# Last two experts added by one-hot products instead of scattered rows, in the tail of a hybrid decoder layer

## The chip, the cores and the metric

The kernel runs on one core of a Trainium2 chip. The metric is the device time in microseconds (us) of one execution. TensorE is called PE below, VectorE DVE, ScalarE ACT, GpSimd POOL and SyncE SP. SP only issues transfers here. "Span" is the time from the first to the last instruction in the profile.

## The reference

One decoder layer over 1024 tokens of width 1024: differential attention and latent attention side by side, cross attention to 256 memory tokens, and a mixture of 32 experts of which each token takes two, all with residual adds, and a final RMSNorm. The change touches only how the experts' rows come back to their tokens, and the final norm:

```python
def block_fn(args):
    tok, wt, e = args
    xb = h_pad[tok]
    hidden = jax.nn.silu(xb @ w_gate[e]) * (xb @ w_up[e])
    return (hidden @ w_down[e]) * wt[:, None].astype(hf.dtype)
...
out = jnp.zeros((n_tok + 1, d), hf.dtype).at[slot_token].add(y.reshape(n_slots, d))[:n_tok]
...
x = x + _hierarchical_moe(...)
return _rms_norm(x, norm_final_g)
```

So the output of a token is the norm of its residual row plus two weighted expert rows.

## The kernel before

All work is recorded first and then ordered by a scheduler written in Python (`Sched`), which emits the instructions of each engine; every scheduled instruction therefore shows the one line L524 (L525 after the change) in the trace, and is told by its tile names. Large tiles (128 rows of 1024 floats, `t4`) share one pool of 50 buffers, and PE writes to 8 PSUM banks.

The experts run one after the other. For expert `e`, POOL gathers the 96 rows of its tokens from DRAM (`xg<-XN,gidx`), PE transposes them and makes the gate and up products (`m_gu`), the hidden rows are transposed (`m_h`), and `m_d` makes the down product of 96 rows by 1024 columns in two banks. ACT scales each bank by the token's weight into the tile `y`, and POOL scatters `y` to a DRAM table `Y` of 2048 rows, two for each token (first and second choice). A scatter waits until the scatter before it has landed, since both write `Y`. The weights come as float32 tiles `eraw`, are split into a high part `ehi` by ACT and a low part `elo` by DVE, and each product is three matmuls in float32r (high by high, high by low, low by high). A plain float32 matmul is used for the first experts' hidden rows (`hw`).

After the last expert `m_end` loads the eight residual tiles (`yt<-XR`). Then the recorded work is flushed and the program comes to an `If` on a count `nov`, of tokens beyond 96 in an expert. With this input `nov` is zero, and the block under the `If` is skipped. Behind it stands the tail: the gain `gfin`, and 16 loads `yt<-Y`, of 512 KB each, the first- and second-choice rows `y0` and `y1` of each of the eight token tiles. The loads go over eight queue semaphores in turn, and SP issues one when the load eight before it has landed. For each tile POOL (tiles 0 to 5) or DVE (6 and 7) adds `y0` to the residual `z`, DVE adds `y1`, ACT squares and sums the row, DVE makes the inverse root in twelve tiny operations for a group of tiles (`rsqrt_mean`, tile `ss`), multiplies by it and by the gain (`scalar_tensor_tensor`), and SP stores the tile.

Of the kernel before, what the change touches and what calls it, by code (L numbers as in the profile page):

```python
# [12 lines left out]
F32 = mybir.dt.float32  # L13
F32R = mybir.dt.float32r
BF16 = mybir.dt.bfloat16
I32 = mybir.dt.int32
AF = mybir.ActivationFunctionType
OP = mybir.AluOpType
# [4 lines left out]
P = 128  # L23
D = 1024
S = 1024
KT = D // P
NT = S // P
# [9 lines left out]
NG, NEG_, NE, FF = 4, 8, 32, 256  # L37
# [18 lines left out]
WHOLE_GU = range(0)  # L56
WHOLE_D = range(4)
WHOLE_PV = ()
TAIL = ((0, 1), (2, 3), (4, 5), (6,), (7,))
TAILV = (6, 7)  # L60
PARK = range(8)
NPRE = 0
NXG = 3
# [10 lines left out]
NS = 96  # L74
# [452 lines left out]
def f32(t):  # L527
    return t.bitcast(F32)
# [30 lines left out]
def hybrid_kernel(ctx: ExitStack, tc: tile.TileContext, a, out):  # L559
    nc = Sched(tc.nc)  # L560
    ctx.enter_context(tc.manual_schedule())
    mm = nc.tensor.matmul

    def mm3(o, ah, al, bh, bl, start, stop):
        mm(o, ah, bh, start=start, stop=False)
        mm(o, ah, bl, start=False, stop=False)
        mm(o, al, bh, start=False, stop=stop)

    def sb(stack, name, bufs=1, side="left"):
        return nc.pool(stack, tc, name, bufs, side=side, reuse_waits="tile")  # L570
# [3 lines left out]
    sm = sb(ctx, "sm")  # L574
# [4 lines left out]
    def bank():  # L579
        return ps.tile([P, 512], F32, tag="b", name="bank", bufs=8)  # L580
# [8 lines left out]
    def t4(name, *shape, dt=F32):  # L589
        v = big.tile(list(shape) or [P, 1024], dt, tag="t4", name=name, bufs=N4)  # L590
        if name == "eraw":
            v.tile.reserve = RESERVE_M
        if name in ("ehi", "elo", "xT", "xw", "hid", "hw", "sg", "y"):
            v.tile.reserve = RESERVE_W
        return v
# [20 lines left out]
    ident = hc[:, 32:160]  # L616
    iota_f = hc[:, 160:288]
# [10 lines left out]
    r = 0  # L628
# [46 lines left out]
    Y = dram.tile([2 * S, D], F32, name="Y")  # L675
# [17 lines left out]
    def two(name):  # L693

        return t4(name, P, 2, CH, dt=F32R)
# [504 lines left out]
    wsl = keep.tile([P, NE], F32, name="wsl")  # L1200
    gidx = keep.tile([P, NE], I32, name="gidx")

    sidx = sums.rearrange("p t h -> p (t h)")[:, 0:NE].bitcast(I32)
# [454 lines left out]
        nc.vector.tensor_copy(nov, obend[:, NE - 1:NE])  # L1658


    w_g, w_u, w_d = (a[n].rearrange("o e d f -> (o e) d f") for n in ("w_expert_gate", "w_expert_up", "w_expert_down"))
    pieces = {}

# [25 lines left out]
    def moe_load(e):  # L1689
        for j in range(6):  # L1690
            moe_piece(e, j)
# [56 lines left out]

    def m_d(e):
        h = st[e]["h"]  # L1750
        y = t4("y")
        for n in range(2):
            yp = bank()
            for k in range(2):
                sl = slice(k * NS, (k + 1) * NS)
                if e in WHOLE_D:
                    mm(yp[0:NS], h[:, 0, sl], pieces[e, 4 + k][:, n], start=k == 0, stop=k == 1)
                else:
                    wh, wl = st[e][4 + k]
                    mm3(yp[0:NS], h[:, 0, sl], h[:, 1, sl], wh[:, n], wl[:, n], k == 0, k == 1)  # L1760
            nc.scalar.activation(y[0:NS, n * 512:(n + 1) * 512], yp[0:NS], AF.Copy, scale=wsl[0:NS, e:e + 1])
        nc.gpsimd.indirect_dma_start(out=Y[:, :], out_offset=Rows(ap=sidx[0:NS, e:e + 1], axis=0), in_=y[0:NS],
                                     in_offset=None, bounds_check=2 * S - 1, oob_is_err=False)

    ys = []

    def m_end():

        for t in range(NT):
            ys.append([t4("yt")])  # L1770
            nc.sync.dma_start(ys[t][0], XR[t * P:(t + 1) * P])
            nc.hold(ys[t][0])

    def experts():
        for e in range(NE + 1):
            if e < NE:
                for i in range(AHEAD):
                    moe_load(e + i)
                m_x(e)
                for j in range(4):  # L1780
                    m_split(e, j)
                moe_load(e + AHEAD)
                if e > 0:
                    m_h(e - 1)
                m_gu(e)
                for j in range(4, 6):
                    m_split(e, j)
            if e > 0:
                if e == NE:
                    m_end()  # L1790
                    m_h(e - 1)
                m_d(e - 1)
# [92 lines left out]
    lazy, nc = nc, tc.nc  # L1885
    mm = nc.tensor.matmul
    A_, obst_, obend_, rank_, nov_, hc_, w3_, XN_, Y_ = (v.real() for v in (A, obst, obend, rank, nov, hc, w3, XN, Y))
# [6 lines left out]
    with tc.If(rnov > 0):  # L1894
# [37 lines left out]
        n = 0  # L1932
        for t in range(NT):
            for k in range(2):
                oh = ohs[n % 2]
# [30 lines left out]
        with tc.For_i(0, rnov, 1) as b:  # L1966
            ev = nc.sync.value_load(bei[0:1, bass.ds(b, 1)], min_val=0, max_val=NE - 1)
            ix = take(1, 2, dt=I32)
            nc.vector.tensor_copy(ix, oidx[:, :, bass.ds(b, 1)].rearrange("p a o -> p (a o)"))
            wx = take(1, 1)  # L1970
            nc.vector.tensor_copy(wx, ow[:, bass.ds(b, 1)])
            wgu = [r4("wgu", P, 2, 512) for _ in range(4)]
            wdn = [r4("wdn") for _ in range(2)]
            for i in range(4):
                for src, o in ((w_g, 0), (w_u, 256)):
                    nc.sync.dma_start(wgu[i][:, :, o:o + 256], src[bass.ds(ev, 1)].rearrange(
                        "o (p k) f -> p (o k) f", k=KT)[:, 2 * i:2 * i + 2])
            for i in range(2):
                nc.sync.dma_start(wdn[i], w_d[bass.ds(ev, 1), i * P:(i + 1) * P].rearrange("o p f -> p (o f)"))
            xg = r4("oxg")  # L1980
            nc.vector.memset(xg, 0.0)
            nc.gpsimd.indirect_dma_start(out=xg, out_offset=None, in_=XN_[:, :],
                                         in_offset=bass.IndirectOffsetOnAxis(ap=ix[:, 1:2], axis=0),
                                         bounds_check=S - 1, oob_is_err=False)
            xT = r4("oxT")
            for g in range(2):
                xp = rbank()
                for k in range(4):
                    o = (4 * g + k) * P
                    nc.tensor.transpose(xp[:, k * P:(k + 1) * P], xg[:, o:o + P], ident_)  # L1990
                nc.vector.tensor_copy(xT[:, g * 512:(g + 1) * 512], xp)
            gu = rbank()
            for k in range(KT):
                mm(gu, xT[:, k * P:(k + 1) * P], wgu[k // 2][:, k % 2], start=k == 0, stop=k == KT - 1)
            sg = take(1, FF)
            nc.scalar.activation(sg, gu[:, 0:FF], AF.Silu)
            nc.vector.tensor_mul(sg, sg, gu[:, FF:2 * FF])
            hp = rbank()
            for k in range(2):
                nc.tensor.transpose(hp[:, k * P:(k + 1) * P], sg[:, k * P:(k + 1) * P], ident_)  # L2000
            hT_ = take(1, 2 * P)
            nc.vector.tensor_copy(hT_, hp[:, 0:2 * P])
            y = r4("oy")
            for n in range(2):
                yp = rbank()
                for k in range(2):
                    mm(yp, hT_[:, k * P:(k + 1) * P],
                       wdn[k][:, n * 512:(n + 1) * 512], start=k == 0, stop=k == 1)
                nc.vector.tensor_scalar(y[:, n * 512:(n + 1) * 512], yp, wx, None, op0=OP.mult)
            nc.gpsimd.indirect_dma_start(out=Y_[:, :], out_offset=bass.IndirectOffsetOnAxis(ap=ix[:, 0:1], axis=0), in_=y,  # L2010
                                         in_offset=None, bounds_check=2 * S - 1, oob_is_err=False)
    nc = lazy


    gf = t4("gfin")
    nc.sync.dma_start(gf, a["norm_final_g"].partition_broadcast(P))
    y_t = Y.rearrange("(t p k) d -> t k p d", p=P, k=2)
    o_t = out.rearrange("o (t p) d -> (o t) p d", p=P)
    for t in range(NT):
        for k in range(2):  # L2020
            ys[t].append(t4("yt"))
            nc.sync.dma_start(ys[t][1 + k], y_t[t, k])

    for tiles in TAIL:
        n = len(tiles)
        ss = carve("ss1")(3, n)
        for i, t in enumerate(tiles):
            z, y0, y1 = ys[t]
            (nc.gpsimd if t not in TAILV else nc.vector).tensor_add(z, z, y0)
            nc.vector.tensor_add(z, z, y1)  # L2030
            nc.scalar.activation(y0, z, AF.Square, accum_out=ss[:, 0, i:i + 1])
        rsqrt_mean(ss[:, 2], ss[:, 0], D, ss[:, 1])
        for i, t in enumerate(tiles):
            z = ys[t][0]
            nc.vector.scalar_tensor_tensor(z, z, ss[:, 2, i:i + 1], gf, op0=OP.mult, op1=OP.mult)
            nc.sync.dma_start(o_t[t], z)
            nc.drop(z)


_INS = ["x", "mem", "positions", "norm_mix_g", "w_in", "diff_lambda_q1", "diff_lambda_k1", "diff_lambda_q2",  # L2040
# [21 lines left out]
```

## Time and profile before

| what | value |
|---|---|
| median of 3 runs | 1236.42 us (1232.04 to 1237.33) |
| profiled execution, its own time | 1232.18 us |
| its span | 1230.0 us |
| mean granted PE clock | 0.945 of full |
| PE, DVE, ACT, POOL busy | 89%, 73%, 65%, 35% of the span |
| bytes moved | 264.95 MB, mean 215 GB/s |

The busy shares are means over stages that differ: PE is nearly always busy until 1166 us and does nothing in the last 64 us. Sums below are made against the span; the profiled execution lies 4.24 us under the median of the runs.

### The profile page before, as it was taken

The numbers are of one execution on the slowest core, as the hardware profiler recorded it, in microseconds if no ns is written. First come the engines' busy times: TensorE is split into PE (matmuls) and PEld (weight loads), VectorE is DVE, ScalarE is ACT, GpSimd is POOL, SyncE is SP. The second block draws the span as 40 slices with busy tenths as digits, with TensorE's granted clock in tenths as the row PEclk, the third lists the DMA queues.
The fourth block names the chain that finished last, engine by engine and source line by source line (L and its number), as shares of the span: only waits on it lengthen the run. The fifth ranks groups of instructions, "written<-read, shape, count | busy, mean of one in ns | idle before, by whom it ended". The sixth has DMA issues, their size and how long they took to land. (4 is left out here: it accounts for less than half of the span.)

```text
span 1230.0 us, 19697 instructions
## 1 busy us (share of the span) xinstructions
PE 1089.7 (89%) x6285; PEld 895.1 (73%) x6285; DVE 895.2 (73%) x2066; ACT 795.8 (65%) x1597; POOL 427.5 (35%) x384
## 2 busy tenths in 40 slices
PE   3999999998788999988999999995999999999800
PEld 2998898897666887678999888884566777766500
DVE  5947535368899879998482566876577889989648
ACT  5735327489888789987362464652676888889702
POOL 2214321158837456957211002153132222221150
PEclk9999999999899999899999999895998999999955
DMA  9118898359845562555440232786999999999983
GB/s 297 34 50 296 309 374 257 123 155 265 198 111 137 143 170 67 136 154 182 155 157 17 69 103 77 254 272 215 326 311 326 339 333 341 342 344 380 365 298 137
DMA packets 147419, 264.95 MB, mean 215 GB/s; under 512 B 17291, under 2 KB 65778, under 8 KB 147314
## 3 DMA queue, kind: packets, MB, share of 16 engines
q1 hardware_dynamic: 131264, 216.61, 55.1%
q0 software_dynamic: 15680, 46.75, 10.9%
q8 instruction: 50, 0.82, 0.3%
q14 instruction: 55, 0.45, 0.1%
q10 hardware_dynamic: 370, 0.32, 0.1%
HBM read 216.96 MB, written 55.05 MB: 221 GB/s over the span
## 5 line engine op out<-in xcount | busy, mean ns | idle before, releaser
L524 DVE TENSOR_TENSOR elo<-eraw,ehi 128x1024 fp32r<-128x1024 f32 x182 | 218.1, 1229 | 36.0 <-ACT ehi L524 28.8
L524 ACT CAST ehi<-eraw 128x1024 fp32r<-128x1024 f32 x184 | 187.2, 1052 | 4.5 <-DMA eraw<-in_w_expert_up_dram 1.9
L524 PE MATMUL bank<-ehi,xT 128*96 128x512 f32 x512 | 170.3, 404 | 2.0 <-ACT y L524 0.5
L524 PE MATMUL bank<-k,q 128*128 128x512 f32 (+5 forms) x480 | 131.0, 383 | 8.4 <-DVE mx L524 2.1
L524 DVE TENSOR_TENSOR pT<-bank,pT 128x512 fp32r<-128x512 f32 (+2 forms) x208 | 108.9, 560 | 24.4 <-ACT pT L524 23.9
L524 PE MATMUL acc<-pT,v 128*128 128x512 f32 (+3 forms) x384 | 114.9, 381 | 11.0 <-DVE pT L524 5.4
L524 PEld LDWEIGHTS bank<-ehi,xT 128*96 128x96 f32 x512 | 83.8, 164 | 39.6 <-ACT y L524 5.7
L524 ACT CAST pT<-bank 128x512 fp32r<-128x512 f32 (+2 forms) x208 | 92.7, 497 | 29.2 <-PE bank L524 28.2
L524 POOL DMA_INDIRECT Y<-y,sums x32 | 36.9, 1154 | 205.3 <-ACT y L524 172.3
L524 PE MATMUL bank<-hc,pt 128*128 128x128 f32 x640 | 98.2, 282 | 10.1 <-POOL pt L524 7.7
L524 PEld LDWEIGHTS bank<-k,q 128*128 128x128 f32 (+1 forms) x480 | 83.9, 198 | 26.1 <-DVE mx L524 8.0
L524 PE MATMUL bank<-elo,xT 128*96 128x512 f32 x256 | 102.0, 399 | 0.3 <-DVE elo L524 0.2
L524 PE MATMUL lbank<-whi,mix 128*128 128x256 f32 x512 | 97.0, 286 | 0.0
L524 PEld LDWEIGHTS bank<-hc,pt 128*128 128x128 f32 x640 | 76.9, 144 | 21.7 <-POOL pt L524 8.7
L524 PE MATMUL lbank<-whi,hT 128*128 128x256 f32 (+1 forms) x384 | 86.7, 311 | 0.0
L524 PEld LDWEIGHTS acc<-pT,v 128*128 128x128 f32 x384 | 65.9, 196 | 27.9 <-DVE pT L524 11.9
L524 PEld LDWEIGHTS lbank<-whi,mix 128*128 128x128 f32 x512 | 81.3, 192 | 0.2
L524 PE MATMUL lbank<-hT,whi 128*128 128x512 f32 x256 | 81.1, 395 | 0.0
L524 PE MATMUL bank<-ehi,hid 128*96 128x512 f32 x224 | 74.7, 394 | 0.8 <-ACT hid L524 0.8
L524 PE MATMUL lbank<-wlo,mix 128*128 128x256 f32 x256 | 72.5, 283 | 0.0
L524 DVE TENSOR_REDUCE mx<-bank 128x1 f32<-128x512 f32 (+3 forms) x112 | 61.0, 568 | 14.7 <-PE bank L524 14.4
L524 POOL TENSOR_TENSOR O<-O,sh 64x512 f32<-64x512 f32 x32 | 41.8, 1307 | 78.4 <-ACT O L524 68.2
(625 smaller groups left out, 2710.1 us busy)
## 6 DMA issues: line engine op xcount, KB each, us to landing
eraw<-in_w_expert_gate_dram SPq DMA_DIRECT2D x128, 256.0 KB
eraw<-in_w_expert_up_dram SPq DMA_DIRECT2D x128, 256.0 KB
eraw<-in_w_expert_down_dram SPq DMA_DIRECT2D x64, 512.0 KB
k<-KD SPq DMA_DIRECT2D x72, 128.0 KB
QM<-st POOLq DMA_DIRECT2D x16, 512.0 KB, 6.4
q<-QM SPq DMA_DIRECT2D x16, 512.0 KB
wraw<-in_w_out_dram SPq DMA_DIRECT2D x16, 512.0 KB
yt<-Y SPq DMA_DIRECT2D x16, 512.0 KB
```

The costliest lines, as they stand in the source:

```text
L524: getattr(getattr(self.nc, eng), name)(*[real(v) for v in a], **{n: real(v) for n, v in k.items()})
```

## The change

Experts 30 and 31 no longer scatter. `m_d` keeps their rows in SBUF as `yl`, a high part (ACT) and a low part (DVE). For each of the two experts and each of the eight token tiles DVE builds a one-hot matrix `oh` (96 rows by 128 tokens, one where the row's token stands), and in the tail PE adds these rows by products of `oh` with `yl`: two experts by two parts by two halves of 512 columns, 8 products for a tile. For the tiles in `TAILP` (1, 3, 4, 6, 7) PE also adds `y0` and `y1`, by float32 products with an identity matrix, 4 more; for tiles 0, 2 and 5 DVE adds them as before. DVE then adds each bank (128 by 512) to the residual. POOL adds nothing in the tail. Since the places of experts 30 and 31 in `Y` are read all the same, `y_zero` writes zeros to them: it is recorded at expert 10, a zeroed tile and two scatters. The 16 loads of `Y` and that of `gfin` stand in `m_end` now, ahead of the `If`; under the `If` the 16 tiles are loaded a second time, since that block writes to `Y`. The tiles are normed in three groups, no longer in five.

```diff
-TAIL = ((0, 1), (2, 3), (4, 5), (6,), (7,))
-TAILV = (6, 7)
+NLAST = 2
+TAIL = ((0, 1), (2, 3, 4), (5, 6, 7))
+TAILP = (1, 3, 4, 6, 7)
...
     def m_d(e):
         h = st[e]["h"]
-        y = t4("y")
+        y = t4("y") if e < NE - NLAST else None
...
-            nc.scalar.activation(y[0:NS, n * 512:(n + 1) * 512], yp[0:NS], AF.Copy, scale=wsl[0:NS, e:e + 1])
+            w = wsl[0:NS, e:e + 1]
+            if e >= NE - NLAST:
+                yl = last[e, n] = two("yl")
+                nc.scalar.activation(yl[0:NS, 0], yp[0:NS], AF.Copy, scale=w)
+                nc.vector.scalar_tensor_tensor(yl[0:NS, 1], yp[0:NS], w, f32(yl[0:NS, 0]), op0=OP.mult, op1=OP.subtract)
+                nc.hold(yl)
+            else:
+                nc.scalar.activation(y[0:NS, n * 512:(n + 1) * 512], yp[0:NS], AF.Copy, scale=w)
+        if e >= NE - NLAST:
+            return
...
+    def y_zero():
+
+        z = t4("y")
+        nc.gpsimd.memset(z[0:NS], 0.0)
+        for e in range(NE - NLAST, NE):
+            nc.gpsimd.indirect_dma_start(out=Y[:, :], out_offset=Rows(ap=sidx[0:NS, e:e + 1], axis=0), in_=z[0:NS],
+                                         in_offset=None, bounds_check=2 * S - 1, oob_is_err=False)
 
     def m_end():
 
         for t in range(NT):
             ys.append([t4("yt")])
             nc.sync.dma_start(ys[t][0], XR[t * P:(t + 1) * P])
-            nc.hold(ys[t][0])
+        for t in range(NT):
+            for k in range(2):
+                ys[t].append(t4("yt"))
+                nc.sync.dma_start(ys[t][1 + k], y_t[t, k])
+            nc.hold(*ys[t])
+        for e in range(NE - NLAST, NE):
+            g = sm.tile([P, 1 + NT], F32, name="lastg", bufs=2)
+            nc.vector.tensor_copy(g[0:NS, 0:1], gidx[0:NS, e:e + 1])
+            oh = last[e] = t4("oh", P, NT, P, dt=F32R)
+            for t in range(NT):
+                nc.vector.tensor_scalar(g[0:NS, 1 + t:2 + t], g[0:NS, 0:1], -float(t * P), None, op0=OP.add)
+                nc.vector.tensor_scalar(oh[0:NS, t], iota_f[0:NS], g[0:NS, 1 + t:2 + t], None, op0=OP.is_equal)
+            nc.hold(oh)
+        last["gf"] = t4("gfin")
+        nc.sync.dma_start(last["gf"], a["norm_final_g"].partition_broadcast(P))
+        nc.hold(last["gf"])
 
     def experts():
         for e in range(NE + 1):
+            if e == 10:
+                y_zero()
...
+        y_t_ = Y_.rearrange("(t p k) d -> t k p d", p=P, k=2)
+        for t in range(NT):
+            for k in range(2):
+                nc.sync.dma_start(ys[t][1 + k].real(), y_t_[t, k])
     nc = lazy
...
             z, y0, y1 = ys[t]
-            (nc.gpsimd if t not in TAILV else nc.vector).tensor_add(z, z, y0)
-            nc.vector.tensor_add(z, z, y1)
+            if t not in TAILP:
+                nc.vector.tensor_add(z, z, y0)
+                nc.vector.tensor_add(z, z, y1)
+            for b in range(2):
+                po = bank()
+                h = slice(b * 512, (b + 1) * 512)
+                m = [(last[e][0:NS, t], last[e, b][0:NS, x]) for e in range(NE - NLAST, NE) for x in range(2)]
+                if t in TAILP:
+                    m = [(ident, y0[:, h]), (ident, y1[:, h])] + m
+                for x, (l, r) in enumerate(m):
+                    mm(po, l, r, start=x == 0, stop=x == len(m) - 1)
+                nc.vector.tensor_add(z[:, h], po, z[:, h])
             nc.scalar.activation(y0, z, AF.Square, accum_out=ss[:, 0, i:i + 1])
```

On SP, at the end of the program before the change, the residual loads are followed by the branch (L1893, L1894), and only behind it stand the gain and the `Y` loads; `DMAHW0` to `DMAHW7` are the eight queue semaphores, `DMASW6` that of a scatter:

```order
L524 DMA yt<-XR 128x1024 [waits DMAHW5_49,DVE_49]
L1893 TENSOR_LOAD nov [waits DVE_49]
L1893 ISA x2
L1894 COMPARE_AND_BRANCH
...
L1894 UNCONDITIONAL_BRANCH [waits SP_sequencer_49,DMAHW0_49,DMAHW1_49,DMAHW2_49,DMAHW3_49,DMAHW4_49,DMAHW5_49,DMAHW6_49,DMAHW7_49]
L524 DMA gfin<-in_norm_final_g_dram 128x1024 [waits DMAHW0_49,DVE_49]
L524 DMA yt<-Y 128x1024 [waits DMASW6_49,DMAHW1_49,DMASW0_49,PE_49]
L524 DMA yt<-Y 128x1024 [waits DMAHW2_49,DVE_49]
```

The same place after it; the rows L2053 are the second loads under the `If`:

```order
L525 DMA yt<-XR 128x1024 [waits DMAHW5_49,DVE_49]
L525 DMA gfin<-in_norm_final_g_dram 128x1024 [waits DMAHW6_49,DVE_49,PE_49]
L525 DMA yt<-Y 128x1024 [waits DMAHW7_49,DMASW6_49,DVE_49]
L525 DMA yt<-Y 128x1024 [waits DMAHW0_49,PE_49]
...
L525 DMA yt<-Y 128x1024 [waits DMAHW6_49,PE_49]
L1931 TENSOR_LOAD nov [waits DVE_49]
...
L2053 DMA yt<-Y 128x1024 x8
...
L1932 UNCONDITIONAL_BRANCH [waits SP_sequencer_49,DMAHW0_49,DMAHW1_49,DMAHW2_49,DMAHW3_49,DMAHW4_49,DMAHW5_49,DMAHW6_49,DMAHW7_49]
L525 DMA out_dram<-yt 128x1024 [waits DMAHW1_49,DVE_49]
```

The 16 loads have moved ahead of the branch and behind one scatter (of expert 29) only. The last branch row is what SP does when the block is skipped: it waits for each queue's own loads, one queue after the other, and then raises that queue's semaphore by what the skipped loads would have added. In the built program the tail's first readers wait for the raised counts: DVE's first add for that of `DMAHW1`, PE's first identity product for those of `DMAHW3` and `DMAHW1`.

PE has nothing behind the branch before the change; after it, these are its first rows there (`yl,oh` a one-hot product, `yt,hc` an identity product):

```order
L525 MATMUL bank<-yl,oh 128x512 x7
L525 MATMUL bank<-yt,hc 128x512
L525 MATMUL bank<-yl,oh 128x512
L525 MATMUL bank<-yt,hc 128x512
L525 MATMUL bank<-yl,oh 128x512 x4
L525 MATMUL bank<-yt,hc 128x512 x2
L525 MATMUL bank<-yl,oh 128x512 x12
```

In all PE has 64 one-hot and 20 identity products there, and the eighth instruction is already an identity product. DVE's rows at the end of the last group of tiles, before and after:

```order
L524 TENSOR_TENSOR yt<-yt 128x1024 x4
L524 TENSOR_SCALAR ss_13714<-ss_13714 128x1 x3
```

```order
L525 SCALAR_TENSOR_TENSOR yt<-yt,ss_13754,gfin 128x1024 x3
L525 TENSOR_TENSOR yt<-bank,yt 128x512 x4
L525 TENSOR_SCALAR ss_13831<-ss_13831 128x3 x3
```

The last adds of a group read a PSUM bank now, and 16 such adds stand in the tail, beside six full adds of `yt<-yt`.

On POOL, among the scatters and gathers of the experts, the two zero scatters stand behind the scatter of expert 8, ahead of the next gather. Before:

```order
L524 DMA xg<-XN,gidx 96x1024
L524 DMA Y<-y,sums 2048x1024
L524 DMA xg<-XN,gidx 96x1024
L524 DMA Y<-y,sums 2048x1024
L524 DMA xg<-XN,gidx 96x1024
```

After:

```order
L525 DMA xg<-XN,gidx 96x1024
L525 DMA Y<-y,sums 2048x1024 x3
L525 DMA xg<-XN,gidx 96x1024
L525 DMA Y<-y,sums 2048x1024
L525 DMA xg<-XN,gidx 96x1024
```

The zeroed tile itself is made by POOL at the start of the program, so it holds one of the 50 buffers until these scatters, and the scheduler orders other work of the attention stages otherwise than before.

## Rows read from the trace of the kernel before

**Rows 1.** Windows: busy us of PE, PEld, DVE, ACT, POOL; PE clock, DMA share, GB/s.

```profile
960.00:1000.00 40.00, 39.68 (x194) 28.14 (x193) 36.13 (x43) 34.59 (x51) 9.80 (x8) 1.00 0.99 335
1150.00:1160.00 10.00, 9.81 (x44) 6.32 (x43) 8.16 (x9) 7.92 (x11) 1.19 (x1) 1.00 1.03 399
1160.00:1170.00 10.00, 5.42 (x24) 3.41 (x22) 1.25 (x3) 2.94 (x5) 0.91 (x1) 0.95 0.67 268
1170.00:1180.00 10.00, 0.00 (x0) 0.00 (x0) 0.00 (x0) 0.00 (x0) 0.91 (x1) 0.50 0.54 159
1180.00:1190.00 10.00, 0.00 (x0) 0.00 (x0) 4.60 (x2) 1.43 (x3) 9.04 (x4) 0.50 1.01 383
```

**Rows 2.** Timeline of POOL at the end: start, us, instruction, idle before and releaser.

```profile
1154.23 1.19 POOL L524 DMA_INDIRECT Y<-y,sums  x1 [7.86 <-ACT y L524]
...
1171.18 0.91 POOL L524 DMA_INDIRECT Y<-y,sums  x1 [7.05 <-DMA Y<-y,sums]
1180.44 2.33 POOL L524 TENSOR_TENSOR yt<-yt 128x1024 f32<-128x1024 f32 x1 [8.34 <-DMA yt<-Y]
```

**Rows 3.** Timeline of SP's issues at the end.

```profile
1150.57 7.97 SPq L524 DMA_DIRECT2D yt<-XR  x8
...
1175.80 14.49 SPq L524 DMA_DIRECT2D yt<-Y  x16
```

**Rows 4.** Timeline of DVE at the end.

```profile
1163.18 0.36 DVE L524 TENSOR_TENSOR hid<-bank,hid 128x192 fp32r<-128x192 f32 x1 [2.28 <-ACT hid L524]
1182.80 1.22 DVE L524 TENSOR_TENSOR yt<-yt 128x1024 f32<-128x1024 f32 x1 [19.27 <-POOL yt L524]
...
1214.36 4.63 DVE L524 TENSOR_TENSOR yt<-yt 128x1024 f32<-128x1024 f32 x4
...
1221.25 0.53 DVE L524 TENSOR_SCALAR ss<-ss 128x1 f32<-128x1 f32 x3
...
1223.44 2.48 DVE L524 SCALAR_TENSOR_TENSOR yt<-yt,ss,gfin 128x1024 f32<-128x1024 f32 x2
```

**Rows 5.** Waits of SP, 1130 to 1230: us in total, times, longest.

```profile
SPq L1894 <- SPq L1894: 11.4, 7, 2.9
```

**Rows 6.** PE: timeline lines, then one group of the lines view (busy us, mean ns).

```profile
850.78 1.54 PE L524 MATMUL bank<-hc,xg 96*128 96x96 f32 x8 [3.04 <-DMA xg<-XN,gidx]
...
867.96 3.60 PE L524 MATMUL bank<-eraw,hw 128*96 128x512 f32 x8
...
1164.44 0.63 PE L524 MATMUL bank<-ehi,hid 128*96 128x512 f32 x2
...
1165.84 0.40 PE L524 MATMUL bank<-ehi,hid 128*96 128x512 f32 x1
...
L524 PE MATMUL bank<-eraw,hw 128*96 128x512 f32 x32 | 14.5, 592 | 0.0
```

**Rows 7.** A group of DVE by form: busy us, mean ns, idle before.

```profile
L524 DVE TENSOR_TENSOR xr<-lbank,xr 128x512 f32<-128x512 f32 x16 | 11.0, 688 | 13.5 <-PE lbank L524 13.2
```

**Rows 8.** Timeline of ACT in the last norm.

```profile
1219.01 1.06 ACT L524 ACTIVATE yt<-yt 128x1024 f32<-128x1024 f32 x1
1219.98 0.19 ACT L524 ACTIVATION_READ_ACCUMULATOR yt<-yt 128x1 f32 x1
```

**Rows 9.** Windows where PE's clock rises after a pause.

```profile
854.00:855.00 1.00, 1.00 (x4) 0.70 (x3) 0.61 (x2) 1.00 (x2) 0.00 (x0) 0.52 0.50 90
855.00:856.00 1.00, 1.00 (x6) 0.69 (x5) 1.00 (x1) 1.00 (x2) 0.00 (x0) 1.00 0.29 119
```

**Rows 10.** Expert loop: scatters and a gather of POOL, then that gather's reader on PE.

```profile
965.70 1.21 POOL L524 DMA_INDIRECT Y<-y,sums  x1 [6.75 <-ACT y L524]
967.22 1.23 POOL L524 DMA_INDIRECT xg<-XN,gidx  x1 [0.31 <-issue]
975.17 1.21 POOL L524 DMA_INDIRECT Y<-y,sums  x1 [6.72 <-ACT y L524]
...
993.01 0.82 PE L524 MATMUL bank<-hc,xg 96*128 96x96 f32 x8
```

More of the change, by code (lines that the diff above doesn't have):

```diff
@@ L1658, in r_over @@
         nc.vector.tensor_copy(nov, obend[:, NE - 1:NE])
+    y_t = Y.rearrange("(t p k) d -> t k p d", p=P, k=2)
     w_g, w_u, w_d = (a[n].rearrange("o e d f -> (o e) d f") for n in ("w_expert_gate", "w_expert_up", "w_expert_down"))
@@ L1765, in hybrid_kernel @@
     ys = []
+    last = {}
+    def y_zero():
[4 more added lines that the diff above has]
+                                         in_offset=None, bounds_check=2 * S - 1, oob_is_err=False)
     def m_end():
@@ L2011, in hybrid_kernel @@
                                          in_offset=None, bounds_check=2 * S - 1, oob_is_err=False)
+        y_t_ = Y_.rearrange("(t p k) d -> t k p d", p=P, k=2)
+        for t in range(NT):
+            for k in range(2):
+                nc.sync.dma_start(ys[t][1 + k].real(), y_t_[t, k])
     nc = lazy
-    gf = t4("gfin")
-    nc.sync.dma_start(gf, a["norm_final_g"].partition_broadcast(P))
-    y_t = Y.rearrange("(t p k) d -> t k p d", p=P, k=2)
+    mm = nc.tensor.matmul
+    gf = last["gf"]
     o_t = out.rearrange("o (t p) d -> (o t) p d", p=P)
[L2019 to L2022, printed above, removed]
     for tiles in TAIL:
@@ L2036, in hybrid_kernel @@
             nc.sync.dma_start(o_t[t], z)
-            nc.drop(z)
+    nc.drop(gf, *[v for y in ys for v in y], *[v for k, v in last.items() if k != "gf"])
 _INS = ["x", "mem", "positions", "norm_mix_g", "w_in", "diff_lambda_q1", "diff_lambda_k1", "diff_lambda_q2",
```

## The prediction

> **What bounds the kernel now.** I read the windows first, then the timelines of the last 70 us, then SP's waits. In the expert loop PE is busy 39.68 of 40 us at full clock while DMA is at 0.99 [rows 1]: the loop belongs to PE, and transfers only just keep up. From 1170 on PE does nothing, and the clock granted to it is 0.50. The end is a chain of other things. PE's last product starts at 1165.84 [rows 6]; POOL issues the last scatter at 1171.18, 7.05 us late, because it waits for the one before it to land [rows 2]; that scatter must land before SP issues the first `Y` load at 1175.80 [rows 3]; the loads run at 383 GB/s [rows 1]; POOL's adds begin at 1180.44, DVE's first at 1182.80 after 19.27 us idle [rows 2, 4]; DVE's last multiplication ends at 1223.44 + 2.48 = 1225.9, 4.1 us ahead of the span's end [rows 4]. The reader is to see a gap of some 17 us between the last product and the first add, and then 43 us of DVE work that POOL feeds slowly.
>
> **The loads.** They wait now for expert 29's scatter alone, issued at 1154.23 [rows 2]. The next one, issued about 9 us later, is what held POOL until 1171.18, so a scatter takes 7 to 8 us to land: 29's is there by 1162. The residual loads are issued by 1158.5 [rows 3]; in 1160 to 1170 DMA is busy 0.67 [rows 1], so I put their end at 1166. One load of 0.524 MB takes 1.31 us at 399 GB/s and 1.37 us at 383 [rows 1]; I take 1.31. The gain goes first: 1167.3. The k-th `Y` load then lands at 1167.3 + 1.31k + about 0.7 for the rest of its flight: the 11th at 1182.4, the 13th at 1185.0, the 16th at 1189. Before, from an issue at 1175.80 and at the same pace, it was about 1198: the loads come some 9 to 10 us earlier.
>
> **The gate.** The gain does not arrive tile by tile. SP spends 11.4 us in seven waits at the skipped block, 2.9 at the longest [rows 5]; today this lies under the wait for the last scatter and costs nothing. After the change the 16 loads stand ahead of that block, which loads them again, so the tail's readers wait for counts that SP raises one queue after the other, each when all loads of that queue have landed. With the gain on queue 6, queue 1 holds the 11th load as its last and queue 3 the 13th. So DVE's first add starts at 1182.4, as late as today, and PE's first identity product, its eighth instruction, at 1185.0. This is the step on which the forecast turns.
>
> **PE in the tail.** A float32r product of 512 columns follows the one before in 0.23 us (two records in 0.63, one in 0.40) [rows 6]. The 64 one-hot products cost 14.9 us, seven of them (1.6 us) ahead of the gate: 13.3 remain. A float32 product appears as two records: 16 calls give 32 records, and eight records take 3.60 us, 0.43 each [rows 6], so 0.86 a call and 17.2 us for 20. Left after the gate: 30.5 us. PE has then stood still for some 13 us, so it begins at the lower clock, which today it has had through the whole tail [rows 1]. The nearest restart is at 850.78 after 3.04 us idle [rows 6]; full clock is back at 855.0 [rows 9], 4.2 us later, of which half is lost: 2.1 us (bounds 0 and 4). Where PE waits for DVE to empty a bank I add 1 us (bounds 0 and 4): with eight banks it can run eight halves ahead. PE ends at 1185.0 + 30.5 + 2.1 + 1 = 1218.6.
>
> **DVE.** Six full adds at 1.16 (four in 4.63), 16 bank adds at 0.69, eight multiplications at 1.24 (two in 2.48), three roots at 1223.44 - 1221.25 = 2.2 [rows 4, 7]: 7.0 + 11.0 + 9.9 + 6.6 = 34.5 us. From 1182.4 this alone would end at 1216.9, so DVE has slack and PE sets the end. Behind PE's last product stand one bank add 0.69, the square 1.06 + 0.19 [rows 8], one root 2.2, three multiplications 3.7 and the last 4.1: 11.9 us.
>
> **Sum.** 1218.6 + 11.9 = 1230.5 against 1230.0. What POOL's adds and the late scatter cost, PE's identity products and the gate take back. POOL's six adds, the first of 2.33 us [rows 2], paced DVE before; without them DVE's adds are taken at 1.16, the pace of the last four.
>
> **What is hidden.** The 16 one-hot comparisons on DVE lie between 0.18 us (the tiny operations, three in 0.53) and 0.36 (the `hid` product of 192 columns) [rows 4]: 2.9 to 5.8 us in the last expert, where DVE has 2.28 us of idle [rows 4]. PE's end moves from 1166.2 by up to 3.5 us; the gate at 1185 covers that with 15 us, and if loads were used as they land it would still be under the 1172 of the third load. The low part of `yl` takes four operations of about 0.7 us on DVE, two after the last product, under the same cover. The zeroed tile is made by POOL early.
>
> **The zero scatters.** Each waits for the one before to land, about 7 us, so POOL's next gather and scatters come some 11 us late and make up about 2.5 us an expert (period 975.17 - 965.70 = 9.5). A gather issued at 967.22 is first read at 993.01 [rows 10], after 25.8 us, of which 6 to 7 are its flight: nearly 20 us of slack. The scatters of the loop move no more bytes in all, but two of them (0.39 MB each) now lie in the loop, where DMA is at 0.99: 0 if prefetch absorbs them, 0.79 MB at 335 GB/s = 2.3 us if not. I take 0.5. The buffer held from the start and the new order in the attention stages are not priced by any row: I allow -4 to +5 and take 0. The span comes to about 1231, the time to 1236.42 + 1 = 1237.4; I say 1237.
>
> **The clock, rule against row.** The mean clock of 0.95 in 1160 to 1170 is one us in ten at 0.50: PE lost its clock at about 1169, some 3 us after its last product [rows 1, 6]. It got it back 4.2 us after the restart at 850.78 [rows 6, 9], which gives the 2.1 above. The Trainium skill (TensorE: Matmul & The Clock Gate, "A second HAM failure mode: psum-queue depth-cycling") warns of more: a kernel that cycles through PSUM banks with short pauses between its groups of products swings between the two clocks. The tail does just that, with DVE emptying eight banks. By this rule the second rival below would hold in part or in full; no row here shows it, since in the loop, where DVE also empties banks, the clock stays at 1.00.
>
> **The rivals.**
> A, the gate does not hold (the readers' counts are met by the first loads, or SP gets through the skipped block early). Then PE's first identity product needs only the third load, 1167.3 + 3.9 + 0.7 = 1171.9, and DVE starts at 1169. PE would end 13 us earlier, at 1205.5; DVE, 1169.3 + 34.5 = 1203.8 plus waits, still fits; the last load at 1189 leaves room. Span 1217.5, time 1224. For: nothing else in the trace is late enough to stop it. Against: SP's 11.4 us of waits in the same place [rows 5].
> B, slower: PE stays at the lower clock in the tail, as it is now there [rows 1]. The 30.5 us become 61, less the 2.1 already counted: span 1259, time 1265. It decides from 12.4 us at the lower clock on (6.2 us lost). Against: from the gate on PE has work without a break, and after 850.78 such work raised the clock [rows 6, 9].
> C, slower: the zero scatters, the held buffer and the new order cost the loop and the attention stages 7 us or more. PE has no idle time there to take it from [rows 1], so each late weight tile shows in full; two scatters' bytes, one scatter chain that reaches a gather's slack, and 5 us of the early stages give 2.3 + 5 to 2.3 + 9, so 1244 to 1248. Against: the gathers' slack [rows 10].
> D, faster: the same two unpriced items help (-4), and PE needs neither restart nor bank waits (-3): 1229.5.
>
> **How the numbers follow.** 0.5% is 6.2 us, about what a measurement of this kernel tells from no change. Forecast (1231 to 1242): 0.48. A 0.2, D 0.07, C 0.17 and B 0.08. Faster 0.27, same 0.48, slower 0.25. The forecast's own range is 1231 to 1242. The range for 8 in 10 leaves out B and the far ends of A and C: 1223 to 1248.
>
> **What would show it.** In the profile of the changed kernel: the `Y` loads issued from about 1162, the last by 1182; PE with seven one-hot products near 1171, then idle until 1185; DVE's first add at 1182; PE busy from 1185 to 1218 with the clock 0.50 for the first few us; DVE's last bank add at 1219 and no POOL work in the tail; the loop's period 9.5 us but for experts 9 to 13. First bank products of tile 1 before 1176 would show A; PE clock of 0.50 beyond 1190, B; a last product of expert 31 later than 1172, C. The forecast is wrong if PE's identity products cost other than 0.86 us each, if DVE rather than PE ends last, or if the gate opens elsewhere.

## The result and the profile after

The change made the kernel slower: 1251.2 us (1249.4 to 1253.22, 4 runs) against 1234.23 us (1230.07 to 1237.33, 4 runs), a ratio of 1.0137 with a 95% interval of 1.0108 to 1.0166. The forecast was 1237 us and no change, with a range up to 1248. The profiled execution has a span of 1251.4 us, 21.4 over that of before. It is the longest of the four runs (1253.22 us), while the profiled execution of before lies under its median, so these 21.4 us between the traces stand for 17.0 between the medians.

Where did they come from? Three points that both traces have split the span: the first scatter, the last product of expert 31, and the end. Before, they lie at 872.56, 1165.84 and 1230.0; after, at 875.31, 1191.82 and 1251.4. From one to the next that is 293.3 and 64.2 us before, 316.5 and 59.6 after. So the expert loop, which the prediction priced at 0.5, took 23.2 us more (the first 2.75 us lie ahead of the experts), and what stands behind PE's last product became 4.6 us shorter. These 4.6 us are no gain. Counted from the scatter of expert 29, for which the `Y` loads wait, the end takes the same in both traces: 1154.23 to 1230.0 and 1175.57 to 1251.4, 75.8 us each. Up to that scatter the loop lost 18.6 us. Behind it PE's last product comes 4.6 us later than before, and that is covered by the loads (`e6_onehot_pool` below). The rows of DVE and PE show where it comes from: the 16 comparisons for the one-hot matrices are made ahead of the last three `elo` splits, and PE waits for one of these.

```profile
1177.67 3.21 DVE L525 TENSOR_SCALAR oh<-hc,lastg 96x128 fp32r<-96x128 f32 x16
1180.81 3.49 DVE L525 TENSOR_TENSOR elo<-eraw,ehi 128x1024 fp32r<-128x1024 f32 x3
```

```profile
1182.08 0.47 PE L525 MATMUL bank<-elo,xT 128*96 128x512 f32 x1 [2.90 <-DVE elo L525]
```

The timeline of POOL after the change shows where in the loop (the scatters of experts 6, 7 and 8, the two of zeros at 974.92 and 983.20, then those of experts 9 and 10):

```profile
942.01 1.19 POOL L525 DMA_INDIRECT Y<-y,sums  x1 [0.30 <-issue]
...
954.18 1.21 POOL L525 DMA_INDIRECT Y<-y,sums  x1 [9.55 <-ACT hid L525]
...
966.06 0.94 POOL L525 DMA_INDIRECT Y<-y,sums  x1 [8.91 <-ACT y L525]
...
974.92 1.83 POOL L525 DMA_INDIRECT Y<-y,sums  x1 [6.11 <-DMA Y<-y,sums]
983.20 0.92 POOL L525 DMA_INDIRECT Y<-y,sums  x1 [6.44 <-DMA Y<-y,sums]
988.59 1.43 POOL L525 DMA_INDIRECT Y<-y,sums  x1 [4.47 <-DMA Y<-y,sums]
...
996.97 1.04 POOL L525 DMA_INDIRECT Y<-y,sums  x1 [4.62 <-ACT y L525]
```

The period of the loop is 9.5 us in [rows 10]; here it is 12.2 and 11.9 us between experts 6 and 8, before any zero scatter is issued. Against the trace of before, expert 4's scatter is 3.0 us late (915.40 against 912.37), expert 8's 9.9 (966.06 against 956.20), expert 11's 21.8 (1006.47 against 984.66), and from there on the lag stays. So there are two losses: about 7 us over experts 4 to 8, and about 12 at the zero scatters. The waits of PE from 870 to 1140 (us, times, longest), before and after, show that PE hardly waited in this loop and now does:

```profile
PE bank L524 <- DMA xg<-XN,gidx: 3.3, 1, 3.3
PE bank L524 <- ACT y L524: 0.5, 1, 0.5
```

```profile
PE bank L525 <- DVE elo L525: 8.3, 1, 8.3
PE bank L525 <- ACT y L525: 5.6, 4, 3.3
PE bank L525 <- DMA xg<-XN,gidx: 3.7, 1, 3.7
```

The one wait for a gather (`xg`) is in both, so it is not the loss. The largest new wait in experts 4 to 8 is for an ACT `y`, which stands right behind a late split on ACT; PE's clock was at 0.50 after it:

```profile
952.28 1.04 ACT L525 CAST ehi<-eraw 128x1024 fp32r<-128x1024 f32 x1 [2.79 <-issue]
```

```profile
953.96 0.74 PE L525 MATMUL bank<-ehi,xT 128*96 128x512 f32 x1 [3.27 <-ACT y L525]
```

```profile
954.00:957.00 3.00, 3.00 (x7) 2.01 (x8) 2.76 (x4) 3.00 (x5) 2.51 (x2) 0.50 1.01 304
```

In the built program this `ehi` takes over the buffer of expert 6's `y` and waits for its scatter, issued at 942.01, and for two weight loads; the trace does not say which came last. In the program of before, that buffer goes to `hid`. The instructions of DVE and PE that waited at the zero scatters show the second loss:

```profile
988.00 3.50 DVE L525 TENSOR_TENSOR elo<-eraw,ehi 128x1024 fp32r<-128x1024 f32 x3 [10.66 <-issue]
```

```profile
989.28 0.74 PE L525 MATMUL bank<-elo,xT 128*96 128x512 f32 x1 [8.27 <-DVE elo L525]
```

PE waits 8.27 us for a split weight, and DVE makes it only at 988.00, just when the second zero scatter has landed (POOL goes on at 988.59). The trace names no releaser for DVE; the built program does: this `elo` waits for the semaphores of both zero scatters, because the scheduler gave it the buffer of the zeroed tile. The windows about it add the clock (columns as in [rows 1]):

```profile
980.00:985.00 5.00, 1.01 (x5) 0.41 (x3) 0.00 (x0) 0.68 (x1) 0.92 (x1) 0.96 0.90 330
985.00:990.00 5.00, 0.72 (x2) 0.57 (x3) 2.00 (x2) 0.00 (x0) 1.41 (x1) 0.50 0.13 45
990.00:995.00 5.00, 5.00 (x14) 3.25 (x13) 3.89 (x6) 1.42 (x4) 2.04 (x2) 0.52 0.77 217
```

PE is idle from 981 to 989 and then works at half clock until nearly 995, some 2.7 us more: together 11 of the 12 us.

The tail went as forecast, counted from the loads. SP's issues, its waits at the skipped block, DVE's first adds and PE's first and last products there:

```profile
1176.69 0.33 SPq L525 DMA_DIRECT2D gfin<-in_norm_final_g_dram  x1
1182.50 16.81 SPq L525 DMA_DIRECT2D yt<-Y  x16
```

```profile
SPq L1932 <- SPq L1932: 9.8, 8, 2.2
```

```profile
1202.78 1.23 DVE L525 TENSOR_TENSOR yt<-yt 128x1024 f32<-128x1024 f32 x1 [9.07 <-SPq L1932]
1208.92 2.36 DVE L525 TENSOR_TENSOR yt<-yt 128x1024 f32<-128x1024 f32 x2 [4.92 <-SPq L1932]
```

```profile
1194.31 1.85 PE L525 MATMUL bank<-yl,oh 96*128 96x512 f32 x7 [2.11 <-DVEq L1932]
1206.40 2.05 PE L525 MATMUL bank<-yt,hc 128*128 128x512 f32 x2 [10.24 <-SPq L1932]
...
1234.60 1.51 PE L525 MATMUL bank<-yl,oh 96*128 96x512 f32 x4
1235.95 1.88 PE L525 MATMUL bank<-yt,hc 128*128 128x512 f32 x4
1237.26 1.50 PE L525 MATMUL bank<-yl,oh 96*128 96x512 f32 x4
```

PE makes seven one-hot products, then stands still until SP has raised the queue's semaphore, and is busy from 1206.40 to 1238.8: 32.4 us where 33.6 were forecast. Its first identity product comes 23.9 us after the issue of the first `Y` load; the forecast had about 23 (1162 to 1185.0). From PE's end to that of the span are 12.6 us, forecast 11.9.

### The profile page after: what moved, and what is told of

The parts are those of the page before. It is cut to its first block, busy times and chain, and to the rows that moved or that the text cites. A ratio compares the mean times of both kernels' runs of the same rounds, so it can differ in the third digit from the quotient of the medians.

```text
span 1251.4 us, 19923 instructions
## 1 busy us (share of the span) xinstructions
PE 1132.0 (90%) x6389; PEld 923.6 (74%) x6389; DVE 893.9 (71%) x2088; ACT 794.2 (63%) x1597; POOL 424.9 (34%) x383
## 5 line engine op out<-in xcount | busy, mean ns | idle before, releaser
L525 PE MATMUL bank<-ehi,xT 128*96 128x512 f32 x512 | 173.3, 410 | 4.7 <-ACT y L525 3.3
L525 PE MATMUL bank<-hc,pt 128*128 128x128 f32 x640 | 101.0, 287 | 8.3 <-DVE mx L525 3.4
L525 PEld LDWEIGHTS bank<-hc,pt 128*128 128x128 f32 x640 | 80.0, 148 | 20.4 <-POOL pt L525 4.2
L525 PE MATMUL bank<-ehi,hid 128*96 128x512 f32 x224 | 77.3, 404 | 3.3 <-ACT y L525 2.3
L525 POOL TENSOR_TENSOR wlo<-wraw,whi 128x1024 fp32r<-128x1024 f32 (+1 forms) x14 | 35.3, 2520 | 95.2 <-ACT whi L525 53.2
```

The costliest lines, as they stand in the source:

```text
L525: getattr(getattr(self.nc, eng), name)(*[real(v) for v in a], **{n: real(v) for n, v in k.items()})
```

## The experiments

Times are medians; each ratio is to the kernel before, which ran beside it.

**The zero scatters early.** The edit of `e1_zero_at_1`:

```diff
-            if e == 10:
+            if e == 1:
                 y_zero()
```

> The two zero scatters are recorded at expert 1 in place of expert 10; nothing else differs from the changed kernel. In its trace PE stands still 8.3 us before an `elo` of expert 10 that reuses the buffer of the zeroed tile, and that waits for the zero scatters to land. Theory 1 (the chain of scatters, and the buffers that it holds, cost the loop 19 us between experts 4 and 10): the scatters land before the first real one is due, the loop keeps its period of 9.5 us, and the time is about 1232. Theory 2 (the zeroed tile made at the start holds a buffer through the attention stages and changes the scheduler's order; the place of the scatters matters little): less than 8 us come back, 1243 to 1250.

1240.39 us, ratio 1.0052 (1.0033 to 1.0071). 10.8 us of the time came back; in the loop it is nearly all. The two zero scatters stand at 846.89 and 855.97, and the loop keeps its period:

```profile
958.47 1.21 POOL L525 DMA_INDIRECT Y<-y,sums  x1 [6.75 <-ACT y L525]
...
967.97 1.21 POOL L525 DMA_INDIRECT Y<-y,sums  x1 [6.75 <-ACT y L525]
...
977.47 1.21 POOL L525 DMA_INDIRECT Y<-y,sums  x1 [6.75 <-ACT y L525]
```

Expert 8's scatter is 2.3 us late and so is that of expert 12, 1.8 of it from the first scatter on, so neither loss is there. From the first scatter to that of expert 29 it takes 283.3 us (874.35 to 1157.60), where the changed kernel takes 300.3 and the one before 281.7: 17 of the 18.6 us are back. Yet not as much came back in the time. From expert 29's scatter to the end it takes 79.6 us in place of 75.8, and behind PE's last product 63.7 (1173.48 to 1237.2), about as long as before the change. SP issues the residual loads 4.3 us ahead of expert 29's scatter here (1153.32), and 8.0 us ahead in the changed kernel (1167.55); the 16 `Y` loads behind them take 20.24 us to issue here and 16.81 there. So in the changed kernel the loads had got ahead of the experts while the loop stood still. Theory 1 holds for the loop, its sum for the end was off.

**The zeroed tile late.** `e2_late_tile` leaves the scatters at expert 10 and makes the tile there:

```diff
+        if e == 8:
+            last["y8"] = y
...
-        nc.gpsimd.memset(z[0:NS], 0.0)
+        nc.gpsimd.tensor_scalar(z[0:NS], last["y8"][0:NS], 0.0, None, op0=OP.mult)
```

> The zero scatters stay at expert 10, but the zeroed tile is made there, by POOL, as the rows of expert 8 times zero, so that no buffer is held from the start. Theory 1: only what the held buffer cost (up to the 7 us lost over experts 4 to 8, before any zero scatter is issued) can come back, the stall of some 12 us at the zero scatters stays: 1244 to 1251. Theory 2: the stages before the experts and the loop fall back into their old order: 1232 to 1240.

1246.91 us, ratio 1.0092 (1.0061 to 1.0122). Expert 8's scatter is 1.3 us late (957.49), expert 11's 13.5 (998.19): the loss over experts 4 to 8 is gone, that at the zero scatters is whole. In the built program an `elo` waits for both zero scatters here too. These are two separate losses, as theory 1 has it.

**The hold alone.** `e3_hold_only` is the kernel before with the tile made at the start and read once expert 8's rows are there:

```diff
+        if e == 8:
+            keep["y8"] = y
...
+    def y_zero():
+
+        z = t4("y")
+        nc.gpsimd.memset(z[0:NS], 0.0)
+        g = sm.tile([P, 1], F32, name="lastg", bufs=1)
+        nc.gpsimd.tensor_add(g[0:NS], z[0:NS, 0:1], keep["y8"][0:NS, 0:1])
...
+            if e == 10:
+                y_zero()
```

> The kernel before, with the zeroed tile alone: made at the start, held until the rows of expert 8 are there, read by one tiny addition of POOL (96 rows by 1), and no zero scatter. Theory 1: at most the 2.8 us of the early stages and the 7 us over experts 4 to 8: 1234 to 1244, no stall of PE over 5 us. Theory 2: most of the 21 us that the loop and the early stages lost: over 1245.

1238.37 us, ratio 1.0032 (1.0018 to 1.0047). From the first scatter to expert 8's it takes 85.4 us (880.04 to 965.42) where 83.6 were needed before: 1.7 us, less than the 7.1 of the changed kernel (875.31 to 966.06 is 90.75), though up to there the tile is held nearly as long. In the built program the same `ehi` waits for expert 6's scatter, but PE stood still for less:

```profile
954.81 0.47 PE L524 MATMUL bank<-ehi,xT 128*96 128x512 f32 x1 [1.32 <-ACT y L524]
```

Theory 2 falls. That the hold makes all of the 7 us does not follow.

**One buffer less.** `e11_before_49` is the kernel before with a smaller pool:

```diff
-N4 = 50
+N4 = 49
```

> The kernel before with 49 buffers in the pool in place of 50. The changed kernel lost 7 us over experts 4 to 8, before any zero scatter was issued, with one buffer held. If one buffer less is enough for that, the loop here loses a like amount or more, since it lasts for all experts: 1241 to 1260. If not, within 3 us of the kernel before, and the 7 us belong to what the zero scatters do to the order.

1257.67 us, ratio 1.0204 (1.0163 to 1.0245): 25 us for one buffer of 50. Two scatters, one expert apart, in the middle of its loop:

```profile
1021.74 0.94 POOL L524 DMA_INDIRECT Y<-y,sums  x1 [7.39 <-ACT y L524]
...
1032.54 1.40 POOL L524 DMA_INDIRECT Y<-y,sums  x1 [8.05 <-ACT hid L524]
```

The period is 10.8 us in place of 9.5. In PE's waits stands what the changed kernel has too:

```profile
PE bank L524 <- ACT y L524: 18.4, 27, 2.3
```

Before, that wait is 0.5 us, once. So over the whole loop the pool has no buffer to spare. Over experts 4 to 8 alone it is another matter: from the first scatter to expert 8's it takes 87.0 us here (879.67 to 966.64), 3.3 more than before, where the changed kernel lost 7.1. One buffer less is thus not shown to be enough for that loss; which tile the scheduler hands on counts too.

**A place of its own for the zeroed tile.** `e9_own_tile`, in the changed kernel:

```diff
-N4 = 50
+N4 = 49
...
-        z = t4("y")
+        z = big.tile([P, 1024], F32, tag="z0", name="y", bufs=1)
```

> The changed kernel with 49 buffers in the pool in place of 50, and the zeroed tile in a place of its own that nothing reuses (the same space in all). If PE's stall of 8.3 us came from the `elo` that takes over the zeroed tile's buffer and so waits for the second zero scatter, no stall of PE over 5 us is left about the zero scatters, and the time is 1238 to 1246 (the pool is one buffer smaller throughout). If the chain of scatters on POOL delays the gathers or the `y` tiles themselves, the stall stays and the time is 1250 or more.

1264.75 us, ratio 1.0253 (1.022 to 1.0287). The wait for `elo` is gone, and another of the same kind has come:

```profile
PE bank L525 <- ACT y L525: 20.4, 29, 3.0
...
ACT ehi L525 <- DMA Y<-y,sums: 11.0, 2, 8.3
...
PE bank L525 <- ACT ehi L525: 6.3, 1, 6.3
```

ACT's `ehi` now waits 8.3 us for a scatter to land: in the built program it takes over the `y` tile of expert 9, whose scatter stands behind the two zero scatters. My expectation of 1238 to 1246 was wrong on both counts: with another tile handed on, the chain of scatters holds up that one, and the smaller pool lengthens the period by some 1.3 us an expert beside it, as in the run above.

**A truer landing time for the scheduler.** `e10_landing_6us`, in the changed kernel:

```diff
-            return {"gpsimd": 1060, "scalar": 60, "sync": 475}[eng], 2500 if "indirect" in name else 950, time
+            return {"gpsimd": 1060, "scalar": 60, "sync": 475}[eng], 6000 if "indirect" in name else 950, time
```

> The changed kernel, but the scheduler's table gives an indirect transfer 6.0 us from issue to landing besides its bytes, in place of 2.5 (the trace shows 6.8 in the median). Nothing else is edited; the order and the choice of buffers follow. If the loop stalls because the scheduler hands on buffers whose scatter is still in flight, most of the 19 us come back: 1232 to 1240. If the stall is in the chain itself, 1247 or more.

1250.62 us, ratio 1.0154 (1.0119 to 1.019): nothing came back in the time. Experts 4 to 8 lost nothing here (expert 8's scatter is 83.4 us behind the first), but the zero scatters' stall stayed, with a wait of PE for `elo` of 8.6 us. In the built program that `elo` takes over expert 9's `y`, as in the run above. That the scheduler thinks a single scatter short is therefore not what makes the stall; that no order could avoid it with this pool is not shown. The first loss is another matter: the zeroed tile is held here as in the changed kernel, and another order lost nothing over experts 4 to 8.

**The gate.** `e4_reload_pool`, in the changed kernel:

```diff
-                nc.sync.dma_start(ys[t][1 + k].real(), y_t_[t, k])
+                nc.gpsimd.dma_start(ys[t][1 + k].real(), y_t_[t, k])
```

> The changed kernel with the second loads under the `If` issued by POOL in place of SP, so that the tail's readers wait for the first loads' own counts, and not for counts that SP raises when each queue has emptied. If the gate held the tail, DVE's first add comes some 10 us earlier after PE's last product, and the time is 1241, 10 under the changed kernel. If PE's 32 us of products or DVE's 34 us set the end whenever they begin, or the loads' bandwidth does, less than 4 us come back.

1241.79 us, ratio 1.0056 (1.0033 to 1.008), 9.4 us under the changed kernel. The loop is as slow as there; the tail takes 47.4 us (1193.50 to 1240.9) in place of 59.6. DVE's first add and PE's first identity product:

```profile
1196.04 1.23 DVE L525 TENSOR_TENSOR yt<-yt 128x1024 f32<-128x1024 f32 x1 [0.65 <-DVEq L1932]
```

```profile
1197.69 1.02 PE L525 MATMUL bank<-yt,hc 128*128 128x512 f32 x2
```

The add comes 2.5 us after PE's last product in place of 11.0. PE keeps its full clock here (two records in 1.02 us, where they took 2.05 after the pause). The gate cost what was expected here.

**Both.** `e5_zero1_reload_pool` has the edits of `e1_zero_at_1` and `e4_reload_pool`.

> Both edits together: zero scatters at expert 1 and the second loads issued by POOL. If the two losses (the loop's stall and the gate) are separate, both gains stand: the tail behind PE's last product, 63.7 us with the zero scatters at expert 1, falls to 47 to 50 (47.4 where the gate alone was taken away), and the time is about 1226, faster than before the change. If the gate only hides that the loads themselves are late when the loop does not stall (the last `Y` load is issued at 1186 there), the tail stays over 55 us and the time over 1231.

1224.75 us, ratio 0.9952 (0.993 to 0.9973): faster than the kernel before. The tail takes 47.6 us (1171.31 to 1218.9). The two gains add up: 0.8% each alone and 1.85% together, by the ratios. A window of the tail, up to PE's last product:

```profile
1176.00:1206.00 30.00, 30.00 (x97) 17.82 (x95) 24.74 (x49) 8.05 (x14) 0.00 (x0) 1.00 0.65 257
```

PE is busy throughout and DVE 24.74 of 30 us: in this stretch the one-hot and identity products are the bound.

**The comparisons on POOL.** `e6_onehot_pool` adds to that:

```diff
-                nc.vector.tensor_scalar(oh[0:NS, t], iota_f[0:NS], g[0:NS, 1 + t:2 + t], None, op0=OP.is_equal)
+                nc.gpsimd.tensor_scalar(oh[0:NS, t], iota_f[0:NS], g[0:NS, 1 + t:2 + t], None, op0=OP.is_equal)
```

> As the run before, and the 16 one-hot comparisons are made by POOL in place of DVE. The last two experts came out 4 to 5 us late in every version that has them on DVE. If it is the comparisons, which stand ahead of the last three `elo` splits on DVE, some 3 to 4 us come back: 1222. If it is the low part of `yl` or the hold of buffers, nothing: 1226.

1225.05 us, ratio 0.9938 (0.9921 to 0.9955), no different from the run before. From expert 29's scatter to the last product it takes 11.7 us (1157.48 to 1169.2), as before the change, where `e5_zero1_reload_pool` needs 15.9: the comparisons did cause that delay. But PE then only waits for the loads:

```profile
1178.03 2.05 PE L525 MATMUL bank<-yt,hc 128*128 128x512 f32 x2 [3.46 <-DMA yt<-Y]
```

Its clock is low there too (two records in 2.05 us): it fell to 0.50 between 1172 and 1173, in the seven products that followed a pause of 2.11 us, and stayed there until 1182. In `e5_zero1_reload_pool` the pause was as long (2.12 us) and the clock stayed at 1.00. So the comparisons lie under the loads, as the prediction had it.

**Groups of 3, 3 and 2.** `e7_groups_332`, on top of `e6_onehot_pool`:

```diff
-TAIL = ((0, 1), (2, 3, 4), (5, 6, 7))
+TAIL = ((0, 1, 2), (3, 4, 5), (6, 7))
```

> As e6, with the tiles normed in groups of 3, 3 and 2 in place of 2, 3 and 3. If PE's last product, one root, and one multiplication for each tile of the last group set the end, one multiplication less (1.24 us) comes off: about 1 us under e6. If DVE is late before PE is through, the larger first group shifts work and nothing is gained.

1223.69 us, ratio 0.9931 (0.991 to 0.9953). The sign is as expected, but 1.4 us lie within the spread of the runs (1220.22 to 1228.81): inconclusive.

**No identity products.** `e8_no_identity`, on top of `e6_onehot_pool`, with `TAILP = ()`.

> As e6, but no tile is in `TAILP`: DVE adds all 16 loaded rows, PE only makes the 64 one-hot products (15 us). By the prices of the rows DVE has 16 x 1.16 + 16 x 0.65 + 9.9 + 6.6 = 45.5 us in place of 34.5: 8 to 11 us slower than e6, about 1231. If the identity products are no help (PE waits on DVE anyway), within 2 us of e6.

1230.29 us, ratio 0.9972 (0.9947 to 0.9997), 5.2 us over `e6_onehot_pool`. So the identity products pay, by about half of what was expected: without them PE waits for DVE to empty its banks:

```profile
1196.78 7.25 PE L525 MATMUL bank<-yl,oh 96*128 96x512 f32 x16 [3.78 <-DVE yt L525]
```

## Why the prediction was wrong

**The step that failed** is that on the zero scatters: "nearly 20 us of slack", and "I take 0.5". It asked who reads the late gathers and how many bytes are moved, and did not ask what else the chain holds. A `y` tile, and the zeroed tile, give their buffer back only when their scatter has landed, and the splits `ehi` and `elo` take those buffers over. Three scatters in a row, each waiting for the one before, keep the zeroed tile until the second zero scatter has landed, and expert 9's rows behind it, in a pool that (`e11_before_49`) has no buffer to spare. That cost 12 us at the scatters (it stays in `e2_late_tile`, is gone in `e1_zero_at_1`), and up to expert 29's scatter the loop lost 18.6 us in place of 0.5. The other term that failed is the held buffer, of which the prediction says "I allow -4 to +5 and take 0": 7 us went over experts 4 to 8, and came back when the tile was not held (`e2_late_tile`). The hold alone cost 1.7 us there (`e3_hold_only`), and in another order nothing (`e10_landing_6us`), so how these 7 us divide between the hold and the scheduler's order stays open. The gathers, the slack of which was right, made PE wait about as before (3.7 us in all, 3.3 before). Of the prediction's list of what would show right or wrong, the period in experts 9 to 13 was looked for in the right place for the second loss, with the wrong reason; the first, at experts 6 to 8, was not on the list.

**Rival C** had the direction and the place, at 0.17, but was priced at 7 to 12 us from bytes and a gather's slack, with 1248 at the most; the loop lost 18.6 up to expert 29's scatter. Its sign, a last product of expert 31 later than 1172, came true (1191.82). The held buffer was "not priced by any row", and that was true of the rows chosen; a look at what each split waits for, in the built program, would have shown which ones take over a tile in flight.

**The gate** was right in place: PE waited for SP until 1206.40. Rival A put its worth at 13 us; taken away it gave back 9.4 us in the changed kernel (`e4_reload_pool`) and 15.6 where the loop has no stall (1240.39 to 1224.75). Rival A, the gate not holding, was rightly put behind it. **PE in the tail** was right in sum: one half of a tile with two identity and four one-hot products takes 2.66 us (1234.60 to 1237.26) where the prices give 2 x 0.86 + 4 x 0.23 = 2.64. **The clock** was right: 0.50 at the restart, back at 1.00 by 1210, 3.6 us after the first identity product, and kept. Rival B did not come true:

```profile
1208.00:1209.00 1.00, 1.00 (x3) 0.67 (x2) 0.08 (x1) 0.00 (x0) 0.00 (x0) 0.50 0.07 29
...
1210.00:1220.00 10.00, 10.00 (x34) 6.14 (x33) 9.40 (x23) 3.45 (x6) 0.00 (x0) 1.00 0.01 2
1220.00:1230.00 10.00, 10.00 (x35) 6.20 (x34) 8.13 (x16) 3.35 (x6) 0.00 (x0) 1.00 0.26 105
```

The prediction set beside rival B the Trainium skill (TensorE: Matmul & The Clock Gate, "A second HAM failure mode: psum-queue depth-cycling"), which tells of a kernel that cycles through PSUM banks and whose PE pauses briefly between groups of products; there the clock swings. This tail does not meet the second condition, though the prediction took it to: from 1210 to 1230 PE is busy 20.00 of 20 us while DVE empties its banks, and the clock stays at 1.00. So the trace does not test that rule. **DVE** (32.7 us busy from 1202 on, 34.5 in the sum) and **the comparisons** (16 in 3.21 us) were right. **The loads** were right in pace, by the 23.9 us from the first issue to PE's first identity product.

Open is the 2.75 us ahead of the first scatter: in single profiles of the kernels here that point lies between 1.2 us earlier and 7.5 us later than before (7.1 later in `e11_before_49`, whose only edit is the pool). `e4_reload_pool` does the same work as the changed kernel up to there, and differs from it by 2.9 us (878.17 against 875.31). So no cause can be read from it.

## What to carry to other kernels

A transfer that is late costs more than its reader: ask which buffer it holds, who takes that buffer next, and how many are spare; in a pool sized to the last buffer, one buffer less lengthened the period of the loop from 9.5 to 10.8 us. When loads are moved ahead of a branch that may load the same tiles again, look at which counts the readers wait for: here, with both loads issued by SP, they waited until each queue had emptied. When two losses are separate, remove them one at a time and then both: here each alone left the change slower, and both together made it 0.5% faster than before.

## What the runs showed of the hardware

Scatters of 96 rows of 4 KB that wait for one another were issued 8.9, 8.3 and 5.4 us apart in the loop, though one takes POOL only 1 to 2 us to issue. A buffer read by such a scatter came free only with its landing, 6.3 to 9.4 us after the issue in the changed kernel (6.9 in the median). A float32 product and the one-hot products behind it are recorded with other starts than the prices suggest: the four float32 records of a half tile take 1.31 us to the next start and the four one-hot products 1.35 (1234.60, 1235.95, 1237.26), where the prices give 1.72 and 0.92. The sum is as forecast.
